# A two-layer streaming encoder on one core: x of the second layer brought into token form by VectorE block transposes and a copy through DRAM, where TensorE transposed it

## The chip, the cores and the metric

The kernel runs on one core of one Trainium2 chip. The core has engines that work side by side, each on its own list of instructions: TensorE (PE in the profile, with its weight loads as PEld), VectorE (DVE), ScalarE (ACT), GpSimd (POOL) and SyncE (SP), which here mostly issues DMA transfers. An engine runs its list in order, and an instruction that waits for another engine or a transfer holds up everything behind it on its own engine. The metric is the device time in microseconds (us) of one execution; lower is better. Where several times are given, the median counts.

## The reference, cut to what matters

The model has two layers on 272 tokens (16 learned ones and 256 of the input) of width 2048. Layer 0 mixes by gated linear attention and stick-breaking attention; layer 1, which the change touches, is a Mamba-2 block (SSD) with 8 groups of 8 heads of 64 channels. All is float32.

```python
proj = einsum('btd,de->bte', h, w_in)              # z, x, B, C and dt of layer 1
xbc = silu(causal_depthwise_conv(xbc, conv_w, conv_b))
dt = softplus(dt_raw + dt_bias)
xdt = x * dt[..., None]                            # per token and head
y = sum over s <= t of (C_t . B_s) * exp(a_cum_t - a_cum_s) * xdt_s   # computed by chunks there
y = rms_norm_groups((y + d_skip * x) * silu(z), norm_w)
out = einsum('bte,ed->btd', y, w_out)              # then residual and layer norm
```

The kernel computes the sum over s without chunks, as one causal matrix per head: M[s, t] = (C_t . B_s) exp(a_cum_t - a_cum_s) for s <= t, and y = xdt^T M. The contraction runs over tokens s, so TensorE wants xdt with tokens on the partitions.

## The kernel before, in words

**Weights and projections.** The weights come in 1 MB tiles `raw` (three buffers), each loaded by one SP transfer (L144) and split in two halves: ScalarE writes the high part `whi` (L159), VectorE, for some halves GpSimd, the low part `wlo` (L160); each has five buffers. A projection is a product of three fp32r matmuls per block (`three`, L178 to L180: high by high, high by low, low by high). A `unit` is 128 output channels of layer 1: 48 matmuls with 256 to 272 columns; the weights are the stationary side, so the result has channels on the partitions and tokens along the row. The output projection runs in units of 24 matmuls with 512 columns (L494 to L496).

**Order of layer 1.** For each group g the units are B, C, four of x and four of z; from group 2 on the four output units of group g-2 follow. Each unit's post-processing is pushed as a small generator task (`push`), and the tasks advance a step at a time between pieces of the projection (`tick`). Their `yield`s therefore decide how many steps later their instructions stand. A simulator of the framework then sets the order on every engine from the written program; all engines keep that order.

**x in a group.** `post_x` runs the convolution (ScalarE and three VectorE steps, L1046 and L1050) from PSUM into `xt` (channels by tokens, 4 blocks of 128 channels). After every second block, `x_path` runs silu (VectorE L1057, three ScalarE steps, VectorE L1061). After the second pair, 12 TensorE transposes follow: 8 of 128x128 (L1173) into two PSUM banks (`po`), and 4 of the last 16 tokens (L1177) into a third bank (`z`). VectorE then multiplies from PSUM by dt (held per token in `est`): four operations of 128x256 (L1186) into `xd`, and four of 16x128 (L1192) into `xd2`.

**The mix.** `mix_ssd` waits for all this and for M, and 32 matmuls (L1235) and 8 small ones (L1241) multiply `xd` by M into two `po` banks. `decay` forms M on VectorE and ScalarE from `ebc`, a copy of the group's cumulated decays on all partitions: 16 subtractions (L1105, L1106; called the M burst below), exponentials, and a product with C.B (L1133). `ebc` is a 1,664 KB transfer (L1072) into the one buffer of the tag `hacc`, so it is loaded once the M burst of the group before has ended. M(g+1)'s burst follows the mix of g.

Of the kernel before, what the change touches and what calls it, by code (L numbers as in the profile page):

```python
# [18 lines left out]
NFIRST = 6  # L19
T = NM + S  # L20
# [10 lines left out]
NG, HPG = 8, 8  # L31
# [51 lines left out]
def _wait(*tasks):  # L83
    for t in tasks:
        while not t.done:
            yield


class _Body:
# [904 lines left out]
    def dt_path(self, ps, scr):  # L994

        nc, lp = self.nc, self.lp
        act, vec = nc.scalar.activation, nc.vector
        H = 64
        while not self.normed:
            yield  # L1000
        m, e, s, s2, p = [scr[:H, i * T : (i + 1) * T] for i in range(5)]
        E = scr[:H, 5 * T : 5 * T + 432]
        bias = self.dta[:, 0:1]
        with self.tc.issue_after(self.last[0]):
            act(e, ps[:H, :T], AF.Abs, bias=bias)
        with self.tc.issue_after(self.last[1]):
            vec.tensor_scalar(m, ps[:H, :T], bias, 0.0, op0=ALU.add, op1=ALU.max)
        act(e, e, AF.Exp, scale=-1.0)

        vec.tensor_scalar(s2, e, 2.0, None, op0=ALU.add)  # L1010
        vec.reciprocal(s2, s2)
        vec.tensor_tensor(s, e, s2, op=ALU.mult)
        vec.tensor_tensor(s2, s, s, op=ALU.mult)
        yield
        vec.tensor_scalar(p, s2, 2.0 / 15, None, op0=ALU.mult)
        for c in (13, 11, 9, 7, 5, 3):
            vec.scalar_tensor_tensor(p, p, 2.0 / c, s2, op0=ALU.add, op1=ALU.mult)
        vec.scalar_tensor_tensor(p, p, 2.0, s, op0=ALU.add, op1=ALU.mult)
        vec.tensor_tensor(m, m, p, op=ALU.add)
        yield  # L1020
        na = lp.tile([H, 1], F32, tag="dt_na", name="dt_na")
        act(na, self.dta[:, 1:2], AF.Exp)
        vec.tensor_scalar(e, m, na, -1.0, op0=ALU.mult, op1=ALU.mult)
        vec.memset(s, 0.0)
        for o, t0 in ((0, 0), (272, 128), (416, 256)):
            vec.tensor_tensor_scan(E[:, o : o + T - t0], e[:, t0:T], s[:, t0:T], 0.0, op0=ALU.add, op1=ALU.add)
        self.edr = self.tc.dram_tile([H, 416], F32, name="edr")
        nc.sync.dma_start(self.edr, E[:, 16:432])
        yield
        self.est = lp.tile([P, 2, 2, H], F32, tag="est", name="est")  # L1030
        self.est2 = lp.tile([16, 2, H], F32, tag="est2", name="est2")
        yield from _wait(self.tasks["res"])
        pt = self.po()
        for n, a in enumerate((E[:, 0:128], E[:, 272:400], m[:, 0:128], m[:, 128:256])):
            nc.tensor.transpose(pt[:, n * H : (n + 1) * H], a, self.ident[:H, :H])
        for n, a in enumerate((E[:, 416:432], m[:, 256:272])):
            nc.tensor.transpose(pt[:16, 256 + n * H : 256 + (n + 1) * H], a, self.ident[:H, :H])
        vec.tensor_copy(self.est.rearrange("p a b h -> p (a b h)"), pt[:, :256])
        vec.tensor_copy(self.est2.rearrange("p a h -> p (a h)"), pt[:16, 256:384])
        yield  # L1040

    def conv(self, src, ct, v, t0=0, lo=0):
# [24 lines left out]
            self.load_decay(g)  # L1067

    def load_decay(self, g):
        eb = self.hp.tile([P, HPG, 416], F32, tag="hacc", name=self.nm("ebc"))  # L1070
        src = self.edr[g * HPG : (g + 1) * HPG, :].rearrange("h c -> (h c)").partition_broadcast(P)
        self.nc.sync.dma_start(eb.rearrange("p h c -> p (h c)"), src)  # L1072
        self.cur["ebc", g] = eb
# [5 lines left out]
    def decay1(self, g):  # L1079
        nc, lp = self.nc, self.lp  # L1080
        act, vec, mm = nc.scalar.activation, nc.vector, nc.tensor.matmul
# [20 lines left out]
        eb = self.cur["ebc", g]  # L1102
# [5 lines left out]
                act(M[:, h - 1 : h + 1, :], M[:, h - 1 : h + 1, :], AF.Exp)  # L1108
                yield
        mt = self.mt  # L1110
        e2 = self.est2[:, 0, g * HPG : (g + 1) * HPG].rearrange("p (h o) -> p h o", o=1).broadcast_to([16, HPG, 16])
        vec.tensor_tensor(mt, eb[:16, :, 400:416], e2, op=ALU.subtract)
        vec.tensor_scalar(mt, mt, 0.0, None, op0=ALU.min)
        act(mt, mt, AF.Exp)
# [5 lines left out]
        pin = self.tc.keep_in_program_order  # L1120
# [10 lines left out]
        for h in range(0, HPG, 2):  # L1131
            c = cb[:, 16:416].rearrange("p (o c) -> p o c", o=1).broadcast_to([P, 2, 400])
            vec.tensor_tensor(M[:, h : h + 2, :], M[:, h : h + 2, :], c, op=ALU.mult)  # L1133
            yield
        c = cb[:16, 0:16].rearrange("p (o c) -> p o c", o=1).broadcast_to([16, 2, 16])
# [16 lines left out]
    def x_path(self, g, j):  # L1152
        nc, vec = self.nc, self.nc.vector
        xt = self.cur["x", g]
        xd = self.cur["xd", g]
        self.silu1(xt[:, j : j + 2, :].rearrange("p a t -> p (a t)"), vec)
        yield
        yield
        yield
        if g == 0:  # L1160
            yield from _wait(self.tasks["dt"])
        if j == 0:
            return
        for _ in range(5):
            yield
        pin = self.tc.keep_in_program_order

        pts = [self.po(), self.po()]
        p2 = self.zbank()
        for pt, jj in zip(pts, (0, 2)):  # L1170
            for i in range(2):
                for t in range(2):
                    pin(nc.tensor.transpose(  # L1173
                        pt[:, t * 256 + i * P : t * 256 + (i + 1) * P], xt[:, jj + i, t * P : (t + 1) * P], self.ident
                    ))
        for i in range(4):
            pin(nc.tensor.transpose(p2[:16, i * P : (i + 1) * P], xt[:, i, 256:T], self.ident))  # L1177
        yield
        hv = lambda a: a.rearrange("p (h c) -> p h c", c=64)
        bd = lambda a: a.rearrange("p (h o) -> p h o", o=1)  # L1180
        for pt, jj in zip(pts, (0, 2)):
            h0 = g * HPG + 2 * jj
            c = slice(jj * P, jj * P + 256)
            for t in range(2):
                d = bd(self.est[:, 1, t, h0 : h0 + 4]).broadcast_to([P, 4, 64])
                vec.tensor_tensor(hv(xd[:, t, c]), hv(pt[:, t * 256 : (t + 1) * 256]), d, op=ALU.mult)  # L1186
            yield
        e2 = bd(self.est2[:, 1, g * HPG : (g + 1) * HPG])
        for j in range(2):
            for p in range(2):  # L1190
                h = 4 * p + 2 * j
                vec.tensor_tensor(  # L1192
                    self.xd2[32 * j : 32 * j + 16, 2 * p : 2 * p + 2, :], hv(p2[:16, :])[:, h : h + 2, :],
                    e2[:, h : h + 2, :].broadcast_to([16, 2, 64]), op=ALU.mult,
                )
        yield

    def post_z(self, ps, g, j):
# [260 lines left out]
```

## Time and profile before

| what | value |
|---|---|
| times of three runs | 1389.19, 1389.46, 1389.4 us; median 1389.4 us |
| the profiled execution | 1389.59 us; span 1387.7 us |
| granted TensorE clock | 1.0 throughout |
| PE busy | 1379.2 us, 99% of the span |
| PEld / DVE / ACT / POOL busy | 1328.3 (96%) / 1017.3 (73%) / 771.7 (56%) / 260.6 us (19%) |
| DMA | 249.83 MB, mean 180 GB/s; the SP queue's packets take 51.0% of 16 engines' span |
| layer 1 | from about 760 us to the end; its x paths run from 767 to 1316 us |

The span is the time between first and last instruction of the profiled execution; its own time is 1.9 us longer. Busy time counts from the start of an instruction to its end, and matmuls overlap, so that the distance between starts, not the duration of one, says what a matmul costs. In rows of groups, "xN" is the count, then busy us and mean ns of one, then the idle time of the engine just before the group's instructions. In rows of the timeline the first two columns are start and duration in us; "x4" joins neighbours; brackets hold the idle time before and what ended it.

### The profile page before, as it was taken

The numbers are of one execution on the slowest core, as the hardware profiler recorded it, in microseconds if no ns is written. First come the engines' busy times: TensorE is split into PE (matmuls) and PEld (weight loads), VectorE is DVE, ScalarE is ACT, GpSimd is POOL, SyncE is SP. The second block draws the span as 40 slices with busy tenths as digits, with TensorE's granted clock in tenths as the row PEclk, the third lists the DMA queues.
The fourth block names the chain that finished last, engine by engine and source line by source line (L and its number), as shares of the span: only waits on it lengthen the run. The fifth ranks groups of instructions, "written<-read, shape, count | busy, mean of one in ns | idle before, by whom it ended". The sixth has DMA issues, their size and how long they took to land.

```text
span 1387.7 us, 26097 instructions
## 1 busy us (share of the span) xinstructions
PE 1379.2 (99%) x10715; PEld 1328.3 (96%) x10715; DVE 1017.3 (73%) x1690; ACT 771.7 (56%) x1149; POOL 260.6 (19%) x253
## 2 busy tenths in 40 slices
PE   9999999999999999999999999999999999999998
PEld 8999999999999999999999999899898999989986
DVE  7857575574565565557899999787877778867687
ACT  6645454454345544556587677565565655656551
POOL 0000010100101000113500153331322323133221
PEclk9999999999999999999999999999999999999999
DMA  8544544445454445544354655465555556455561
GB/s 320 185 161 156 181 154 171 163 156 179 156 179 156 153 152 179 174 151 148 122 199 169 251 202 201 158 256 174 213 180 187 197 187 228 164 200 185 179 216 61
DMA packets 38007, 249.83 MB, mean 180 GB/s; under 512 B 4288, under 2 KB 6144, under 8 KB 9472
## 3 DMA queue, kind: packets, MB, share of 16 engines
q1 hardware_dynamic: 37168, 247.38, 51.0%
q8 instruction: 84, 1.38, 0.4%
q10 hardware_dynamic: 720, 0.79, 0.2%
q14 instruction: 35, 0.29, 0.1%
HBM read 245.94 MB, written 2.20 MB: 179 GB/s over the span
## 4 chain that ended last, share of the span: by engine, by line
PE 94%; DVE 3%; DMA 1%; ACT 1%; POOL 1%; issue 0%; SPq 0%; ACTq 0%; POOLq 0%; DVEq 0%
PE pj L179 25%; PE pj L178 25%; PE pj L180 25%; PE pj L494 4%; PE pj L496 4%; PE pj L495 4%; PE po L1235 1%; PE po L608 1%; DVE wlo L160 1%; PE po L1173 0%; DMA raw<-in_wts 0%; PE po L587 0%; PE z L1123 0%; POOL yu L1246 0%; DVE M L1105 0%
## 5 line engine op out<-in xcount | busy, mean ns | idle before, releaser
L178 PE MATMUL pj<-xhi,whi 128*128 128x272 f32 (+4 forms) x2560 | 732.1, 286 | 1.3 <-DVE fix L936 0.5
L179 PE MATMUL pj<-xlo,whi 128*128 128x272 f32 (+4 forms) x2560 | 730.8, 286 | 0.0
L180 PE MATMUL pj<-xhi,wlo 128*128 128x272 f32 (+4 forms) x2560 | 730.1, 286 | 0.0
L159 ACT ACTIVATE whi<-raw 128x1024 fp32r<-128x1024 f32 (+2 forms) x434 | 449.6, 1039 | 423.8 <-PE pj L179 350.7
L160 DVE TENSOR_TENSOR wlo<-raw,whi 128x1024 fp32r<-128x1024 f32 (+2 forms) x405 | 503.3, 1247 | 242.0 <-ACT whi L159 237.4
L178 PEld LDWEIGHTS pj<-xhi,whi 128*128 128x128 f32 x2560 | 482.1, 189 | 3.7 <-ACT whi L159 0.9
L179 PEld LDWEIGHTS pj<-xlo,whi 128*128 128x128 f32 x2560 | 482.1, 188 | 1.5 <-DVE wlo L160 0.4
L180 PEld LDWEIGHTS pj<-xhi,wlo 128*128 128x128 f32 x2560 | 481.9, 188 | 1.0 <-issue 0.8
L178 PE MATMUL pj<-mixh,whi 128*128 128x272 f32 x384 | 110.5, 289 | 0.0
L180 PE MATMUL pj<-mixh,wlo 128*128 128x272 f32 x384 | 110.5, 288 | 0.0
L179 PE MATMUL pj<-mixl,whi 128*128 128x272 f32 x384 | 110.4, 288 | 0.0
L160 POOL TENSOR_TENSOR wlo<-raw,whi 128x1024 fp32r<-128x1024 f32 x29 | 73.0, 2517 | 192.6 <-ACT whi L159 192.6
L494 PE MATMUL pj<-whi,yh 128*128 128x512 f32 (+1 forms) x240 | 93.3, 389 | 0.0
L495 PE MATMUL pj<-wlo,yh 128*128 128x512 f32 (+1 forms) x240 | 92.6, 386 | 0.0
L496 PE MATMUL pj<-whi,yl 128*128 128x512 f32 (+1 forms) x240 | 92.2, 386 | 0.0
L261 POOL TENSOR_TENSOR gr<-gr,gsc 128x1088 f32<-128x1088 f32 x6 | 15.4, 2568 | 308.2 <-ACT gsc L260 308.2
L179 PEld LDWEIGHTS pj<-mixl,whi 128*128 128x128 f32 x384 | 72.3, 188 | 0.2
L180 PEld LDWEIGHTS pj<-mixh,wlo 128*128 128x128 f32 x384 | 72.3, 188 | 0.1
L178 PEld LDWEIGHTS pj<-mixh,whi 128*128 128x128 f32 x384 | 72.2, 188 | 0.1
L503 DVE SCALAR_TENSOR_TENSOR acc<-pj,rr,acc 128x512 f32<-128x512 f32 (+1 forms) x65 | 46.5, 734 | 13.9 <-PE pj L496 13.9
L496 PEld LDWEIGHTS pj<-whi,yl 128*128 128x128 f32 x240 | 45.1, 188 | 9.1
L494 PEld LDWEIGHTS pj<-whi,yh 128*128 128x128 f32 x240 | 45.1, 188 | 9.0
(351 smaller groups left out, 1472.2 us busy)
## 6 DMA issues: line engine op xcount, KB each, us to landing
raw<-in_wts SPq DMA_DIRECT2D x212, 1024.0 KB, 4.8
ebc<-edr SPq DMA_DIRECT2D x8, 1664.0 KB, 6.7
raw<-in_wts SPq DMA_DIRECT2D x9, 256.0 KB, 6.4
hacc<-in_xT SPq DMA_DIRECT2D x7, 272.0 KB, 5.3
early<-in_wts SPq DMA_DIRECT2D x2, 512.0 KB, 6.5
lg<-in_lnr SPq DMA_DIRECT2D x1, 1024.0 KB, 4.7
lb<-in_lnr SPq DMA_DIRECT2D x1, 1024.0 KB, 5.3
out_h<-acc SPq DMA_DIRECT2D x2, 384.0 KB, 2.4
```

The source lines that it names most:

```text
L159: self.nc.scalar.activation(hi, src, AF.Copy)
L160: eng.tensor_tensor(lo, src, hi.bitcast(F32), op=ALU.subtract)
L178: mm(ps, whi, xhi, start=first, stop=False)
L179: mm(ps, whi, xlo, start=False, stop=False)
L180: mm(ps, wlo, xhi, start=False, stop=last)
L261: mul(c, c, e, op=ALU.mult)
L494: mm(ps, yh[:, kk, tt], hi[:, k, :], start=kk == 0, stop=False)
L495: mm(ps, yh[:, kk, tt], lo[:, k, :], start=False, stop=False)
L496: mm(ps, yl[:, kk, tt], hi[:, k, :], start=False, stop=kk == 3)
L503: self.nc.vector.scalar_tensor_tensor(a, ps, r[:, t : t + 1], a, op0=ALU.mult, op1=ALU.add)
L608: mm = lambda r, a, b, start=False, stop=False: self.nc.tensor.matmul(o[:, r], a, b, start=start, stop=stop, skip_group_check=True)
L1235: pin(mm(ov[p][i * 64 : (i + 1) * 64, jj, t0:S], xd[:, s, h * 64 : (h + 1) * 64], M[:, h, c0:c1], start=(s, jj) == (0, 0), stop=False, **gk,))
```

## The change

`x_path` no longer uses TensorE. After each pair's silu, VectorE transposes `xt` in blocks of 32x32, each within itself: one instruction for 256 tokens of two blocks (L1171, 128 partitions x 512 elements), and one for the columns of the last tokens (L1172, 128 x 64). A block's inside is then token by channel, but each block of 32 tokens still lies on the partitions of its channels. So SP writes the result to DRAM (L1179, 512 KB in rows of 4 KB; L1180, 64 KB) and reads it back with tokens on the partitions: four transfers of 128 KB in pieces of 512 bytes (L1183), two of 32 KB in pieces of 128 bytes straight into `xd2` (L1187). VectorE then multiplies by dt from SBUF: four operations of 128x4x64 (L1199), two of 16x256 in place on `xd2` (L1206).

The room for the blocks is the last 1,024 floats per partition of the buffer that holds `ebc`. So `x_path` waits until `ebc` of its group is allocated, and the load of `ebc` of the next group waits until L1199 has read the blocks back. The waits for dt and five `yield`s are gone. `est2` stands on two partition ranges. M, the mix and everything else is unchanged, though the lines are 1 to 11 numbers higher: L1061 is L1062, L1072 is L1075, L1105/L1106 are L1108/L1109, L1235/L1241 are L1246/L1252.

```diff
--- before.py
+++ after.py
@@ -1028,7 +1028,7 @@
         nc.sync.dma_start(self.edr, E[:, 16:432])
         yield
         self.est = lp.tile([P, 2, 2, H], F32, tag="est", name="est")
-        self.est2 = lp.tile([16, 2, H], F32, tag="est2", name="est2")
+        self.est2 = lp.tile([48, 2, H], F32, tag="est2", name="est2")
         yield from _wait(self.tasks["res"])
         pt = self.po()
         for n, a in enumerate((E[:, 0:128], E[:, 272:400], m[:, 0:128], m[:, 128:256])):
@@ -1036,7 +1036,8 @@
         for n, a in enumerate((E[:, 416:432], m[:, 256:272])):
             nc.tensor.transpose(pt[:16, 256 + n * H : 256 + (n + 1) * H], a, self.ident[:H, :H])
         vec.tensor_copy(self.est.rearrange("p a b h -> p (a b h)"), pt[:, :256])
-        vec.tensor_copy(self.est2.rearrange("p a h -> p (a h)"), pt[:16, 256:384])
+        for q in (0, 32):
+            vec.tensor_copy(self.est2[q : q + 16].rearrange("p a h -> p (a h)"), pt[:16, 256:384])
         yield
 
     def conv(self, src, ct, v, t0=0, lo=0):
@@ -1067,7 +1068,9 @@
             self.load_decay(g)
 
     def load_decay(self, g):
-        eb = self.hp.tile([P, HPG, 416], F32, tag="hacc", name=self.nm("ebc"))
+        eb = self.hp.tile([P, KT * T], F32, tag="hacc", name=self.nm("ebc"))
+        self.cur["xs", g] = eb[:, HPG * 416 :].rearrange("p (b c x) -> p b c x", c=4, x=32)
+        eb = eb[:, : HPG * 416].rearrange("p (h c) -> p h c", h=HPG)
         src = self.edr[g * HPG : (g + 1) * HPG, :].rearrange("h c -> (h c)").partition_broadcast(P)
         self.nc.sync.dma_start(eb.rearrange("p h c -> p (h c)"), src)
         self.cur["ebc", g] = eb
@@ -1108,7 +1111,7 @@
                 act(M[:, h - 1 : h + 1, :], M[:, h - 1 : h + 1, :], AF.Exp)
                 yield
         mt = self.mt
-        e2 = self.est2[:, 0, g * HPG : (g + 1) * HPG].rearrange("p (h o) -> p h o", o=1).broadcast_to([16, HPG, 16])
+        e2 = self.est2[:16, 0, g * HPG : (g + 1) * HPG].rearrange("p (h o) -> p h o", o=1).broadcast_to([16, HPG, 16])
         vec.tensor_tensor(mt, eb[:16, :, 400:416], e2, op=ALU.subtract)
         vec.tensor_scalar(mt, mt, 0.0, None, op0=ALU.min)
         act(mt, mt, AF.Exp)
@@ -1157,42 +1160,50 @@
         yield
         yield
         yield
-        if g == 0:
-            yield from _wait(self.tasks["dt"])
+        while ("ebc", g) not in self.cur:
+            yield
+
+        xs = self.cur["xs", g]
+        lp = self.lp
+        if j == 0:
+            self.cur["x9", g] = lp.tile([P, 4, 32], F32, tag="x9", name=self.nm("x9"))
+        x9 = self.cur["x9", g]
+        vec.transpose(xs[:, :, j : j + 2, :].rearrange("p b c x -> p c b x"), xt[:, j : j + 2, :S].rearrange("p c (b x) -> p c b x", x=32))
+        vec.transpose(x9[:, j : j + 2, :], xt[:, j : j + 2, 240:T])
+        yield
         if j == 0:
             return
-        for _ in range(5):
-            yield
-        pin = self.tc.keep_in_program_order
-
-        pts = [self.po(), self.po()]
-        p2 = self.zbank()
-        for pt, jj in zip(pts, (0, 2)):
+
+        d = self.tc.dram_tile([4, 32, 8, P], F32, name=self.nm("xdr"))
+        d9 = self.tc.dram_tile([4, 32, 4, 32], F32, name=self.nm("xdr9"))
+        nc.sync.dma_start(d.rearrange("p t b x -> (p t) (b x)"), xs.rearrange("q b c x -> q (b c x)"))
+        nc.sync.dma_start(d9.rearrange("p t c x -> (p t) (c x)"), x9.rearrange("q c x -> q (c x)"))
+        xb = xs.rearrange("q b c x -> q (b c x)").rearrange("q (s p x) -> q s p x", s=2, p=4)
+        for b in range(4):
+            nc.sync.dma_start(
+                xb[32 * b : 32 * b + 32], d[:, :, b::4].rearrange("p t s x -> t s p x")
+            )
+        for i in range(2):
+            nc.sync.dma_start(
+                self.xd2[32 * i : 32 * i + 16].rearrange("t (n a) (b x) -> t n (a b) x", n=2, b=2),
+                d9[:, 16:, i::2].rearrange("p t n x -> t n p x"),
+            )
+        yield
+        yield
+
+        for t in range(2):
             for i in range(2):
-                for t in range(2):
-                    pin(nc.tensor.transpose(
-                        pt[:, t * 256 + i * P : t * 256 + (i + 1) * P], xt[:, jj + i, t * P : (t + 1) * P], self.ident
-                    ))
-        for i in range(4):
-            pin(nc.tensor.transpose(p2[:16, i * P : (i + 1) * P], xt[:, i, 256:T], self.ident))
-        yield
-        hv = lambda a: a.rearrange("p (h c) -> p h c", c=64)
-        bd = lambda a: a.rearrange("p (h o) -> p h o", o=1)
-        for pt, jj in zip(pts, (0, 2)):
-            h0 = g * HPG + 2 * jj
-            c = slice(jj * P, jj * P + 256)
-            for t in range(2):
-                d = bd(self.est[:, 1, t, h0 : h0 + 4]).broadcast_to([P, 4, 64])
-                vec.tensor_tensor(hv(xd[:, t, c]), hv(pt[:, t * 256 : (t + 1) * 256]), d, op=ALU.mult)
-            yield
-        e2 = bd(self.est2[:, 1, g * HPG : (g + 1) * HPG])
-        for j in range(2):
-            for p in range(2):
-                h = 4 * p + 2 * j
-                vec.tensor_tensor(
-                    self.xd2[32 * j : 32 * j + 16, 2 * p : 2 * p + 2, :], hv(p2[:16, :])[:, h : h + 2, :],
-                    e2[:, h : h + 2, :].broadcast_to([16, 2, 64]), op=ALU.mult,
-                )
+                o = xd[:, t, :].rearrange("q (c i a x) -> q c i a x", c=4, i=2, a=2)[:, :, i]
+                x = xb[:, t, 2 * i : 2 * i + 2].rearrange("q a (c x) -> q c a x", c=4)
+                e = self.est[:, 1, t, g * HPG + i : (g + 1) * HPG : 2].rearrange("q (c o u) -> q c o u", o=1, u=1)
+                vec.tensor_tensor(o, x, e.broadcast_to([P, 4, 2, 32]), op=ALU.mult)
+            yield
+        for i in range(2):
+            q = slice(32 * i, 32 * i + 16)
+            x = self.xd2[q].rearrange("t (n h) c -> t n h c", n=2)
+            e = self.est2[q, 1, g * HPG : (g + 1) * HPG].rearrange("t (n j h) -> t j n h", n=2, j=2)[:, i]
+            e = e.rearrange("t n (h u) -> t n h u", u=1)
+            vec.tensor_tensor(x, x, e.broadcast_to([16, 2, 2, 64]), op=ALU.mult)
         yield
 
     def post_z(self, ps, g, j):
```

What this moves is shown at three places. First TensorE in group 3, within the unit of the block `pj`, before:

```order
L180 MATMUL pj_11389<-xhi,wlo_11331 128x256
L1173 MATMUL po_11406<-ident,xt_11029 128x128 x4
L1173 MATMUL po_11407<-ident,xt_11029 128x128 x4
L1177 MATMUL z_64<-ident,xt_11029 16x128 x4
L178 MATMUL pj_11389<-xhi,whi_11330 128x256
```

and with the change at the same place of that unit:

```order
L180 MATMUL pj_11406<-xhi,wlo_11334 128x256
L178 MATMUL pj_11406<-xhi,whi_11333 128x256
L179 MATMUL pj_11406<-xlo,whi_11333 128x256
L180 MATMUL pj_11406<-xhi,wlo_11334 128x256
L178 MATMUL pj_11406<-xhi,whi_11333 128x256
```

The 12 transposes are gone from the middle of the unit, and nothing stands in their place.

Second, VectorE in group 3 from the second silu on (L1061 before, L1062 now; L160 are weight splits, L1057/L1058 begin the silu of z). Before:

```order
L1061 TENSOR_TENSOR xt_11029<-xt_11029,xcl_11279 128x544
L160 TENSOR_TENSOR wlo_11441<-raw_11327,whi_11440 128x1024
L160 TENSOR_TENSOR wlo_11479<-raw_11387,whi_11478 128x1024
L1057 TENSOR_SCALAR xcl_11420<-gz_11325 128x512
L1186 TENSOR_TENSOR xd_11030<-po_11406,est 128x256 x2
L1186 TENSOR_TENSOR xd_11030<-po_11407,est 128x256 x2
L1192 TENSOR_TENSOR xd_8126<-z_64,est_8718 16x128 x4
L160 TENSOR_TENSOR wlo_11507<-raw_11387,whi_11506 128x1024
L160 TENSOR_TENSOR wlo_11540<-raw_11475,whi_11539 128x1024
L160 TENSOR_TENSOR wlo_11587<-raw_11535,whi_11586 128x1024
```

With the change:

```order
L1062 TENSOR_TENSOR xt_11027<-xt_11027,xcl_11280 128x544
L1171 STREAM_TRANSPOSE ebc_10878<-xt_11027 128x2x8x32
L1172 STREAM_TRANSPOSE x_1359_11185<-xt_11027 128x64
L160 TENSOR_TENSOR wlo_11476<-raw_11404,whi_11475 128x1024
L1058 TENSOR_SCALAR xcl_11425<-gz_11328 128x512
L160 TENSOR_TENSOR wlo_11504<-raw_11404,whi_11503 128x1024
L160 TENSOR_TENSOR wlo_11537<-raw_11472,whi_11536 128x1024
L1199 TENSOR_TENSOR xd_11028<-ebc_10878,est 128x4x64 x4
L1206 TENSOR_TENSOR xd_8126<-xd_8126,est_8718 16x256 x2
L160 TENSOR_TENSOR wlo_11584<-raw_11532,whi_11583 128x1024
L1058 TENSOR_SCALAR xcl_11546<-gz_11328 128x512
```

The two transposes stand right behind the silu, and three weight splits later the multiplies; the split behind them is queued after whatever they wait for.

On SP the same stretch now reads (`raw` are weight tiles, `xdr` the copies in DRAM, and L1187's target is `xd2`); before there were only weight tiles in it:

```order
L144 DMA raw_11532<-in_wts 128x2048
L1179 DMA xdr_11349<-ebc_10878 128x1024
L1180 DMA xdr_1379_11350<-x_1359_11185 128x128
L144 DMA raw_11579<-in_wts 128x2048
L1183 DMA ebc_10878<-xdr_11349 32x8x128 x4
L1187 DMA xd_8126<-xdr_1379_11350 16x8x32 x2
L144 DMA raw_11661<-in_wts 128x2048
L1075 DMA ebc_11821<-edr 128x3328
L144 DMA raw_11707<-in_wts 128x2048
```

A weight tile stands between the write and the reads, another behind the reads, and then comes the decay copy of group 4, which stood far ahead of these rows before.

Third, VectorE in group 1, with the change, behind the second transposes and up to the multiplies (L1051 are steps of a convolution, L266 to L268 a row statistic):

```order
L160 TENSOR_TENSOR wlo_10026<-raw_9873,whi_10025 128x1024
L266 TENSOR_TENSOR rt_9435<-rr_9436 128x2
L1051 SCALAR_TENSOR_TENSOR bc_9866<-pj_9800,cpk,bc_9866 128x270
L267 SCALAR_TENSOR_TENSOR rt_9435<-rt_9435,rm_9434 128x2
L1051 SCALAR_TENSOR_TENSOR bc_9866<-pj_9800,cpk,bc_9866 128x269
L268 SCALAR_TENSOR_TENSOR rr_9436<-rt_9435,rr_9436 128x2
L160 TENSOR_TENSOR wlo_10063<-raw_9980,whi_10062 128x1024
L1051 SCALAR_TENSOR_TENSOR bc_9866<-pj_9875,cpk,bc_9866 128x256 x3
L1058 TENSOR_SCALAR xcl_10007<-bc_9866 128x528
L1199 TENSOR_TENSOR xd_9242<-ebc_9081,est 128x4x64 x4
L1206 TENSOR_TENSOR xd_8126<-xd_8126,est_8718 16x256 x2
```

The multiplies stood in front of the splits of `raw_9873` and the steps of this convolution before; now they are behind both, and the mix of group 1 stands about two and a half units later on TensorE than before.

More of the change, by code (lines that the diff above doesn't have):

```diff
@@ L1162, in x_path @@
+        yield
         if j == 0:
             return
-        for _ in range(5):
-            yield
-        pin = self.tc.keep_in_program_order
-        pts = [self.po(), self.po()]
-        p2 = self.zbank()
-        for pt, jj in zip(pts, (0, 2)):
-            for i in range(2):
-                for t in range(2):
-                    pin(nc.tensor.transpose(
-                        pt[:, t * 256 + i * P : t * 256 + (i + 1) * P], xt[:, jj + i, t * P : (t + 1) * P], self.ident
-                    ))
@@ new lines, in x_path @@
+        yield
[6 more added lines that the diff above has]
+                vec.tensor_tensor(o, x, e.broadcast_to([P, 4, 2, 32]), op=ALU.mult)
+            yield
+        for i in range(2):
+            q = slice(32 * i, 32 * i + 16)
[3 more added lines that the diff above has]
+            vec.tensor_tensor(x, x, e.broadcast_to([16, 2, 2, 64]), op=ALU.mult)
```

## The prediction

> **What bounds the kernel now.** I read the page first: the busy times and the chain of waits.
>
> ```profile
> PE 1379.2 (99%) x10715; PEld 1328.3 (96%) x10715; DVE 1017.3 (73%) x1690; ACT 771.7 (56%) x1149; POOL 260.6 (19%) x253
> PE 94%; DVE 3%; DMA 1%; ACT 1%; POOL 1%; issue 0%; SPq 0%; ACTq 0%; POOLq 0%; DVEq 0%
> ```
>
> TensorE is busy for 99% of the span and is 94% of the chain that ends last, so what leaves TensorE's list should leave the time, as long as nothing else takes its place. Since shares are averages, the second view is the table of busy time by window (columns: length, then PE, PEld, DVE, ACT, POOL, granted clock, DMA share, GB/s). Groups 0 to 2 form their x in the first of these windows, groups 3 to 7 in the second.
>
> ```profile
> 760.00:900.00 140.00, 139.79 (x1139) 131.90 (x1139) 127.80 (x244) 93.52 (x143) 47.91 (x35) 1.00 0.57 202
> 900.00:1340.00 440.00, 440.00 (x3269) 412.73 (x3268) 336.97 (x518) 258.11 (x360) 123.75 (x93) 1.00 0.56 195
> ```
>
> TensorE has no gap in either, at full clock. VectorE has 12.2 us free of 140 in the first and 103 of 440 in the second. The early stretch is therefore where VectorE could become the bound, and it gets work from this change.
>
> **What leaves TensorE.** The timeline of PE around group 3's transposes (start, duration, then the line):
>
> ```profile
> 956.38 1.04 PE L1173 MATMUL po<-ident,xt 128*128 128x128 f32 x8
> 957.25 0.60 PE L1177 MATMUL z<-ident,xt 128*16 128x128 f32 x4
> 957.61 0.37 PE L178 MATMUL pj<-xhi,whi 128*128 128x256 f32 x1
> 957.81 0.28 PE L179 MATMUL pj<-xlo,whi 128*128 128x256 f32 x1
> 957.93 0.28 PE L180 MATMUL pj<-xhi,wlo 128*128 128x256 f32 x1
> ```
>
> Matmuls overlap, so I count from start to start. From 956.38 to 957.81 there are 12 transposes and one L178; a matmul of this unit is worth 957.93 - 957.81 = 0.12 us. The transposes cost 1.43 - 0.12 = 1.31 us, and eight groups 10.5 us. Bounds: the pitch alone, (957.25 - 956.38) / 8 = 0.109 us, times 96 is 10.4 us; where a group's transposes stand in two places, the slow step behind them (957.81 - 957.61 - 0.12 = 0.08 us) comes twice, 11.1 us in all. I take 10.5 us.
>
> **What VectorE loses and gets.** Its timeline in group 3, from the second silu to the M burst, brackets being idle time:
>
> ```profile
> 954.05 0.73 DVE L1061 TENSOR_TENSOR xt<-xt,xcl 128x544 f32<-128x544 f32 x1 [0.37 <-ACT xcl L1060]
> 957.67 1.41 DVE L1186 TENSOR_TENSOR xd<-po,est 128x256 f32<-128x256 f32 x4
> 959.00 0.96 DVE L1192 TENSOR_TENSOR xd<-z,est 16x128 f32<-16x128 f32 x4
> 960.25 1.23 DVE L160 TENSOR_TENSOR wlo<-raw,whi 128x1024 fp32r<-128x1024 f32 x1 [0.29 <-ACT whi L159]
> 963.01 1.23 DVE L160 TENSOR_TENSOR wlo<-raw,whi 128x1024 fp32r<-128x1024 f32 x1 [1.54 <-ACT whi L159]
> 968.40 1.23 DVE L160 TENSOR_TENSOR wlo<-raw,whi 128x1024 fp32r<-128x1024 f32 x1 [4.16 <-ACT whi L159]
> 971.25 1.23 DVE L160 TENSOR_TENSOR wlo<-raw,whi 128x1024 fp32r<-128x1024 f32 x1 [1.29 <-ACT whi L159]
> 977.11 0.35 DVE L1105 TENSOR_SCALAR M<-ebc,est 128x256 f32<-128x256 f32 x1 [1.49 <-PE po L1235]
> 983.08 1.21 DVE L160 TENSOR_TENSOR wlo<-raw,whi 128x1024 fp32r<-128x1024 f32 x1
> ```
>
> L1186 and L1192 leave: 1.41 + 0.96 = 2.4 us. For what comes, the nearest rows are groups by shape (count, busy us, mean ns):
>
> ```profile
> L1057 DVE TENSOR_SCALAR xcl<-gz 128x512 f32<-128x512 f32 x16 | 6.7, 419 | 0.0
> L1061 DVE TENSOR_TENSOR xt<-xt,xcl 128x544 f32<-128x544 f32 x15 | 12.3, 820 | 11.9 <-ACT xcl L1060 11.7
> L1105 DVE TENSOR_SCALAR M<-ebc,est 128x256 f32<-128x256 f32 x64 | 30.0, 469 | 7.0 <-PE po L1235 7.0
> ```
>
> No block transpose is in the trace. One of 128x512 should lie between 0.42 us (L1057, as many elements) and 0.82 us (L1061); I take 0.5, two are 1.0 us. The two of 64 columns I take at 0.2 each, below the 0.24 us of one L1192 (0.96 / 4). The four L1199 have 256 elements like L1186, 0.35 to 0.47 us each; at 0.4, 1.6 us. Two L1206 at 0.35, 0.7 us. Together 3.7 us, bounds 3.0 and 4.9. VectorE gets 1.3 us more per group (0.6 to 2.5). In groups 3 to 7 that costs nothing: the idle times in brackets above are 9.1 us in this one group. Without that cover it would be 1.3 us of time per group.
>
> [...]
>
> **The way through DRAM, on the clock of group 3.** The durations come from the DMA issues (KB each, median us from issue to landing), the deadlines from PE and SP rows:
>
> ```profile
> raw<-in_wts SPq DMA_DIRECT2D x212, 1024.0 KB, 4.8
> ebc<-edr SPq DMA_DIRECT2D x8, 1664.0 KB, 6.7
> raw<-in_wts SPq DMA_DIRECT2D x9, 256.0 KB, 6.4
> out_h<-acc SPq DMA_DIRECT2D x2, 384.0 KB, 2.4
> edr<-dt_scr SPq DMA_DIRECT2D x1, 104.0 KB, 2.1
> ```
>
> ```profile
> 974.13 2.93 PE L1235 MATMUL po<-M,xd 128*64 128x256 f32 x32
> 983.18 0.33 SPq L1072 DMA_DIRECT2D ebc<-edr  x1
> 988.59 0.39 PE L495 MATMUL pj<-wlo,yh 128*128 128x512 f32 x1
> ```
>
> - The silu ends at 954.05 + 0.73 = 954.8; the second transposes (0.5 + 0.2) at 955.5.
> - The write of 512 KB takes between 2.4 us (`out_h`, 384 KB) and 6.4 us (256 KB behind others). I take 4.0, nearer to half a weight tile: 959.5, at the latest 961.9.
> - The reads stand behind a weight tile on SP. Its buffer is freed by the split at 960.25, so it leaves at 961.5, and the reads right behind it.
> - Six reads bring 576 KB. Alone, 2.1 us (`edr`). In turn, each with its own 2.1 us behind a tile of 4.8 us, 17.4 us. I take them as bytes in the stream of the tile: (1024 + 576) / 1024 x 4.8 = 7.5 us, because weight tiles of 1 MB land in 4.8 us though the DMA engines are busy 0.56 of that window. They land at 969.0 (963.6 to 979.3).
> - L1199 and L1206 take 2.3 us: xd is ready at 971.3. The mix starts at 974.1: 2.8 us to spare; at the upper end 7.5 us late.
>
> Queued behind L1199 on VectorE is a weight split. It would have started at 968.40 and now starts at 971.3, 2.9 us late. The tightest split I quote, that at 983.08, ends at 984.3 and is first used by TensorE at 988.59, 4.3 us later. So the wait is covered, by 1.4 us; once the cover is gone each us is one on TensorE. On SP, behind the reads, wait weight tiles and then the decay copy of group 4, which now also waits for L1199 (end 970.6): it lands at 970.6 + 6.7 = 977.3, and the M burst that needs it began at 977.11. Before, a copy left at 983.18, at the end of one burst, for a burst a whole group later. The burst, and the split at 983.08 behind it, come 0.2 us late, up to 2 us if the copy shares with a tile; both within the 4.3 us. I cost groups 3 to 7 at nothing, and I see that two covers are thin.
>
> **Groups 0 to 2.** Here VectorE has 12.2 / 3 = 4.1 us free per group, and it must take 1.3 us of work and the same sort of wait at L1199, up to the 2.9 us of group 3: 4.2 us. That just does not fit. The mixes of groups 0 and 1 stand later on TensorE, which takes the pressure off xd but not off the splits. Bounds: no loss, and three waits of 2.9 us uncovered, 8.7 us. I take 1.5 us, since before these waits there are more splits in VectorE's order than in group 3, and a later wait is a shorter one.
>
> **Sum.** The profiled execution took 1389.59 us, span 1387.7 us and 1.9 us around it, 0.2 us over the median of 1389.4. 1389.59 - 10.5 + 1.5 = 1380.6; against the median, 1380.4 us.
>
> **Rivals.**
>
> *VectorE keeps half of the early stretch.* For it: 91% busy there. Against it: the wait falls behind more work. Half of 8.7 us: 1389.4 - 10.5 + 4.35 = 1383.3 us.
>
> *The gain is eaten.* All three early waits are uncovered (8.7 us) and the thin covers of groups 3 to 7 give a little: 1389.4 - 10.5 + 8.7 = 1387.6 us and up to 1392, no difference that counts.
>
> *The round trip is late at every mix: slower.* The place is L1199, behind the reads on SP. TensorE's list reaches the mix, xd is not there, and the eight mixes each wait. It decides from 10.5 / 8 = 1.3 us late per group, that is, when the reads land 4.1 us later than I take them. Half way between my value (2.8 us early) and the upper end (7.5 us late) is 2.4 us late: 1389.4 - 10.5 + 8 x 2.4 = 1398.1 us; by the upper end, 1439. For it: the reads are in pieces of 512 and 128 bytes where weight tiles come in rows of 8 KB, and 256 KB of weights took 6.4 us while 1 MB took 4.8, so bytes are not what always decides. Against it: six transfers that are issued at once need not run in turn.
>
> [...]
>
> *The change doesn't do what it says.* The orders of PE exclude it: the transposes are gone and nothing is added.
>
> **Chances and range.** A difference under 0.2% (2.8 us) can't be told from none. My forecast (1378 to 1382.5) 0.47, the half loss 0.17, the gain eaten 0.09, slower 0.24. Below 1378, with the 11.1 us bound and nothing lost early, 0.03. So faster 0.03 + 0.47 + 0.17 = 0.67, within 0.2% 0.09, slower 0.24. Up to 1395 the slower case is half included, so the range 1378 to 1395 leaves out 0.12 above and 0.03 below. The likeliest's own range is 1378 to 1382.5.
>
> **What would show it.** PE rows without L1173 and L1177, and no gap ahead of L1246 in any group: then the sum holds. In the waits, PE L1246 waiting for L1199 or L1206 by over 1 us shows the slower rival. The split behind L1199 and the idle time that VectorE spends before L1199 show the size of the wait; I expect about 3 us in groups 3 to 7. M bursts that begin later than the mix's end with a DMA of `ebc` as their releaser show the second thin cover. PE idle before L180 (released by `wlo`) between 760 and 900 shows the early loss. My number is wrong if the reads take over 11 us, or if VectorE's transposes take over 1.5 us each.

## The result

The changed kernel takes 1396.1 us (median; 1392.1 to 1400.8), the kernel before 1389.24 us (1388.6 to 1390.1) in runs beside it. The ratio is 1.0054, interval 1.0038 to 1.0070: slower by 6.9 us, where 9 us less were forecast. Besides, the time now varies by nearly 9 us from run to run; before it varied by 1.5 us.

The profiled execution is the fastest of the changed kernel's, 1392.13 us (span 1390.2 us), 2.5 us over the one of before. Its page, busy times and chain:

```profile
PE 1371.7 (99%) x10619; PEld 1321.0 (95%) x10619; DVE 1029.6 (74%) x1707; ACT 771.7 (56%) x1149; POOL 254.8 (18%) x253
PE 87%; DVE 6%; DMA 4%; issue 1%; ACT 1%; POOL 0%; SPq 0%; ACTq 0%; DVEq 0%; POOLq 0%
```

The transposes did leave: TensorE has 96 instructions fewer and is busy for 7.5 us less. But it is 87% of the chain where it was 94%; VectorE has grown from 3% to 6% of it and DMA from 1% to 4%. By window, as in the prediction:

```profile
760.00:900.00 140.00, 134.53 (x1082) 127.53 (x1082) 126.13 (x232) 89.81 (x137) 36.89 (x32) 0.99 0.65 219
900.00:1340.00 440.00, 434.80 (x3217) 407.14 (x3216) 347.38 (x542) 259.29 (x361) 126.97 (x95) 1.00 0.61 210
```

TensorE, with a gap of 0.2 us in all before, now stands still for 5.5 us in the first window and 5.2 us in the second. The timeline of PE holds it in five waits (the bracket is the wait and what ended it):

```profile
816.91 0.40 PE L178 MATMUL pj<-xhi,whi 128*128 128x272 f32 x1 [1.76 <-ACT gz L1213]
841.75 0.62 PE L1246 MATMUL po<-M,xd 128*64 128x256 f32 x2 [2.30 <-DVE xd L1199]
893.80 3.17 PE L1246 MATMUL po<-M,xd 128*64 128x256 f32 x32 [1.41 <-DVE xd L1199]
908.65 0.47 PE L494 MATMUL pj<-whi,yh 128*128 128x512 f32 x1 [2.27 <-DVE acc L503]
1079.32 0.47 PE L494 MATMUL pj<-whi,yh 128*128 128x512 f32 x1 [2.93 <-DVE acc L503]
```

They sum to 10.7 us. Two of the five are waits for x at a mix, as the prediction's slower rival has them. The first is for ScalarE, which has to empty a PSUM bank of z; the last two are for VectorE, which has to empty a bank of the output projection.

There is a further loss that the waits don't show. Windows around 842 us:

```profile
838.00:842.00 4.00, 1.70 (x14) 1.42 (x12) 0.82 (x3) 2.41 (x4) 1.30 (x1) 1.00 0.88 282
842.00:846.00 4.00, 4.00 (x21) 2.31 (x20) 3.94 (x7) 0.00 (x0) 0.00 (x0) 0.57 0.63 216
846.00:850.00 4.00, 4.00 (x44) 3.74 (x40) 2.57 (x7) 1.16 (x3) 1.43 (x2) 1.00 0.97 403
```

Right after the wait of 2.30 us TensorE's granted clock is 0.57 for 4 us, by which I estimate another 4 x 0.43 = 1.7 us: the last 30 matmuls of this mix take 4.46 us, all 32 of group 2's 3.17. So 1389.59 - 10.5 + 10.7 + 1.7 = 1391.5 us, near the 1392.13 us of this execution. It is the only one with a trace, so the 4.0 us from it to the median are not accounted for; the mean clock does not order the times, since three executions at 0.999 took 1394.1 to 1395.0 us, five at 0.995 or 0.996 took 1396.1 to 1400.8, and this one had 0.998.

**Where each wait comes from.** First the one at 816.91, followed back over VectorE, GpSimd and ScalarE:

```profile
808.96 0.46 DVE L1256 SCALAR_TENSOR_TENSOR yu<-xt,cpk,po 128x256 f32<-128x256 f32 x1
809.57 3.53 POOL L1257 TENSOR_TENSOR yu<-yu,gz 128x256 f32<-128x256 f32 x1 [6.45 <-DVE yu L1256]
813.14 0.51 ACT L1259 ACTIVATE yh<-yu,cpk 128x256 fp32r<-128x256 f32 x1 [3.16 <-POOL yu L1257]
816.50 0.88 ACT L1213 ACTIVATE gz<-pj 128x256 f32<-128x256 f32 x3
```

After group 0's mix VectorE computes yu, late, since its list is full (from 795 to 820 us it has no idle time); GpSimd and then ScalarE wait for it in their lists; the emptying of z's banks stands behind that on ScalarE; TensorE has no free bank. No transfer is in this chain. But L1257 on GpSimd also takes 3.53 us where 0.74 is its median: the 2.8 us more are longer than the wait at the end of the chain, and why it took so long was not tested. Next the mix of group 1, on SP and VectorE:

```profile
825.63 0.33 SPq L1179 DMA_DIRECT2D xdr<-ebc  x1
832.36 3.34 SPq L1183 DMA_DIRECT2D ebc<-xdr  x4
841.17 1.43 DVE L1199 TENSOR_TENSOR xd<-ebc,est 128x256 f32<-128x256 f32 x4 [5.11 <-DMA ebc<-xdr]
```

The write leaves at 825.63, the reads at 832.36, the multiplies start at 841.17: 15.5 us. VectorE waits 5.1 us for them, with its list full behind. Last the wait at 908.65, by way of the decay copy:

```profile
894.69 0.33 SPq L1075 DMA_DIRECT2D ebc<-edr  x1
901.25 2.36 DVE L1108 TENSOR_SCALAR M<-ebc,est 128x256 f32<-128x256 f32 x1 [1.33 <-DMA ebc<-edr]
907.77 1.39 DVE L503 SCALAR_TENSOR_TENSOR acc<-pj,rr,acc 128x512 f32<-128x512 f32 x2
```

The copy for group 3 leaves when L1199 of group 2 has ended (894.69), the M burst waits for it until 901.25, and the evictions L503 stand behind the burst. TensorE needs their bank. This wait is thus made by the change in group 2; only the one at 1079.32 is made by a later group.

### The profile page after: what moved, and what is told of

Its sections match the earlier page's. It is cut to its first block, busy times and chain, and to the rows that moved or that the text cites. A ratio compares the mean times of both kernels' runs of the same rounds, so it can differ in the third digit from the quotient of the medians.

```text
span 1390.2 us, 25999 instructions
## 1 busy us (share of the span) xinstructions
PE 1371.7 (99%) x10619; PEld 1321.0 (95%) x10619; DVE 1029.6 (74%) x1707; ACT 771.7 (56%) x1149; POOL 254.8 (18%) x253
## 4 chain that ended last, share of the span: by engine, by line
PE 87%; DVE 6%; DMA 4%; issue 1%; ACT 1%; POOL 0%; SPq 0%; ACTq 0%; DVEq 0%; POOLq 0%
PE pj L179 24%; PE pj L178 24%; PE pj L180 24%; PE pj L494 3%; PE pj L496 3%; PE pj L495 3%; PE po L608 1%; DMA ebc<-xdr 1%; PE po L1246 1%; DMA ebc<-edr 1%; DMA xdr<-ebc 1%; DVE wlo L160 1%; DVE M L1108 1%; DVE M L1109 0%; POOL yu L1257 0%
## 5 line engine op out<-in xcount | busy, mean ns | idle before, releaser
L180 PE MATMUL pj<-xhi,wlo 128*128 128x272 f32 (+4 forms) x2560 | 729.6, 285 | 0.0
L160 DVE TENSOR_TENSOR wlo<-raw,whi 128x1024 fp32r<-128x1024 f32 (+2 forms) x405 | 504.8, 1250 | 226.4 <-ACT whi L159 225.3
L180 PEld LDWEIGHTS pj<-xhi,wlo 128*128 128x128 f32 x2560 | 482.0, 188 | 0.3
L180 PE MATMUL pj<-mixh,wlo 128*128 128x272 f32 x384 | 110.5, 288 | 0.0
L160 POOL TENSOR_TENSOR wlo<-raw,whi 128x1024 fp32r<-128x1024 f32 x29 | 74.5, 2569 | 168.2 <-ACT whi L159 168.2
L180 PEld LDWEIGHTS pj<-mixh,wlo 128*128 128x128 f32 x384 | 72.3, 188 | 0.1
L495 PEld LDWEIGHTS pj<-wlo,yh 128*128 128x128 f32 x240 | 45.1, 188 | 8.6
```

The source lines that it names most:

```text
L160: eng.tensor_tensor(lo, src, hi.bitcast(F32), op=ALU.subtract)
L180: mm(ps, wlo, xhi, start=False, stop=last)
L495: mm(ps, yh[:, kk, tt], lo[:, k, :], start=False, stop=False)
```

## The experiments

All times are medians; ratios are to the kernel before, run beside. In every run the simulator sets the order of all engines anew, so an edit can also move instructions that it does not touch.

**1. The transposes alone.** The kernel before without them; VectorE multiplies x as it lies:

```diff
-        pts = [self.po(), self.po()]
-        p2 = self.zbank()
...
-        vec.tensor_tensor(hv(xd[:, t, c]), hv(pt[:, t * 256 : (t + 1) * 256]), d, op=ALU.mult)
+        vec.tensor_tensor(f(hv(xd[:, t, c])), x, f(d), op=ALU.mult)   # x is a part of xt
```

> The kernel before, with the 12 transposes of every group left out and nothing put in their place: VectorE multiplies x as it lies (channels on the partitions), so x reaches the mix untransposed. It measures the first term of the prediction alone. By the prediction's rows the transposes cost 10.5 us (bounds 10.4 to 11.1), so 1389.2 - 10.5 = 1378.7 us (1378 to 1379.5). If the PE time that leaves is taken up again by another engine (VectorE in the early groups, weights), it comes out above 1382 us, and the loss in the changed kernel would not be the transfers' alone.

1382.9 us (1380.2 to 1384.2; ratio 0.9953, 0.9938 to 0.9967). The gain is 6.3 us, not 10.5, though no work was added to any engine. Its waits of PE:

```profile
PE po L1250 <- POOL ysq L1244: 1.8, 1, 1.8
PE pj L178 <- ACT gz L1191: 0.7, 1, 0.7
```

Both lie between 815 and 830 us, where TensorE stands still for 2.56 us and the granted clock is 0.77 on the mean:

```profile
815.00:830.00 15.00, 12.44 (x74) 11.82 (x74) 13.47 (x21) 11.69 (x23) 4.39 (x4) 0.77 0.61 210
```

By that I estimate at most 15 x 0.23 = 3.45 us more. TensorE is faster by itself in the early groups and runs into the engines that follow it. The gain went with the mean clock: of the four executions the shortest, at 1.0, gained 9.0 us, the longest, at 0.998, 5.0 us.

**2. No way through DRAM.** The changed kernel without write, read back and the last tokens:

```diff
-        nc.sync.dma_start(d.rearrange(...), xs.rearrange(...))
-        nc.sync.dma_start(d9.rearrange(...), x9.rearrange(...))
...
-        for b in range(4):
-            nc.sync.dma_start(xb[32 * b : 32 * b + 32], d[:, :, b::4].rearrange("p t s x -> t s p x"))
```

> The changed kernel with the way through DRAM left out: no write, no read back; VectorE transposes the blocks and multiplies them where they lie, so x reaches the mix with its blocks unmoved and the last tokens are left out. Theory: the changed kernel loses its gain to waits for the way through DRAM (TensorE at the mixes of groups 1 and 2, and the decay copy that waits for the multiplies, so the M burst and then the evictions of the output units come late). Without the transfers 1378 to 1382 us. Rival: VectorE's own new work (transposes of 0.70 us where 0.5 was expected) makes it the bound in the early groups: then 1386 us or more, with TensorE waiting for VectorE between 800 and 910 us.

1389.7 us (ratio 1.0004, 0.9994 to 1.0013): nothing is gained, so my theory of the transfers fell. The rival held in its time, but TensorE waits for ScalarE and not for VectorE itself. The one large wait of PE, and what stands behind it on GpSimd and ScalarE:

```profile
PE pj L178 <- ACT gz L1200: 9.2, 1, 9.2
```

```profile
819.39 1.57 POOL L1244 TENSOR_TENSOR yu<-yu,gz 128x256 f32<-128x256 f32 x1 [10.85 <-DVE yu L1243]
825.35 1.21 ACT L1200 ACTIVATE gz<-pj 128x256 f32<-128x256 f32 x4 [3.54 <-POOL yu L1244]
```

It is the wait of 816.91 again, now 9.2 us long, with VectorE's yu at its root. Without a single transfer the early groups eat the whole gain of eight groups.

**3. The decay copy parted from the blocks.** One lasting buffer, of which `ebc` and the blocks are two parts, so that the copy no longer waits for L1199:

```diff
-        eb = self.hp.tile([P, KT * T], F32, tag="hacc", name=self.nm("ebc"))
+        if g == 0:
+            self.eball = self.hp.tile([P, KT * T], F32, tag="hacc", name="ebc")
+        eb = self.eball
```

> The changed kernel with ebc and the blocks as two parts of one lasting buffer, so that the decay copy of group g+1 waits only for the M burst of group g, as in the kernel before, and no longer for L1199; all else as changed. Theory: the two waits of TensorE for evictions (L494 for L503, 2.3 and 2.9 us in the profile) go, the two at the mixes of groups 1 and 2 (2.3 and 1.4 us) stay: 5.2 us less than the changed kernel's 1396.1, so about 1391 us (1388 to 1393). Rival, that these waits come from VectorE's load or from DMA traffic in general: no change, 1395 to 1397 us.

1394.4 us (1392.4 to 1397.6; ratio 1.0037, 1.0026 to 1.0049). That is 1.7 us less than the changed kernel, but the intervals overlap, and it lies above the expected range. The wait for evictions falls from 5.2 to 1.4 us, while the wait behind ScalarE is 6.1 us here; alone the run doesn't settle the price of the copy.

**4. The change in groups 3 to 7 alone.**

```diff
-            self.tasks["x", g, j] = self.push(self.x_path(g, j - 1))
+            self.tasks["x", g, j] = self.push((self.x_path_old if g < 3 else self.x_path)(g, j - 1))
```

> The change in groups 3 to 7 alone; groups 0 to 2 use TensorE as before. Theory: five eighths of the 10.5 us leave (6.6 us), the waits at 817, 842, 894 and 909 us in the profile go, that at 1079 us (2.9 us) stays: 1389.2 - 6.6 + 2.9 = 1385.5 us (1383 to 1389). Rival, that the loss is spread over all eight groups: five eighths of the whole loss of 6.9 us, 1393.5 us.

1386.5 us (1383.0 to 1390.8; ratio 0.9982, 0.9971 to 0.9992): faster than before by 2.6 us, as expected. The profiled execution, at 1390.8 us the longest of the ten, waits twice for evictions:

```profile
PE pj L494 <- DVE acc L503: 5.0, 2, 2.5
```

**5. The same with the decay copy parted** (the edits of 3 and 4 together).

> The change in groups 3 to 7 alone, and the decay copy parted from the blocks, so that it waits for the M burst of the group before alone. Theory: what the change in groups 3 to 7 alone still loses (1386.5 us against 1389.2 - 6.6 = 1382.6) is the late decay copy: two waits of TensorE of 2.5 us for evictions behind the M burst, and the lowered clock behind each. Parted, 1382.5 to 1384 us. Rival, that the loss is in DMA traffic or in the wait at L1199: it stays at 1386 us or more.

1383.9 us (1382.7 to 1384.8; ratio 0.9961, 0.9946 to 0.9976). This beats both kernels: 5.5 us under the one before. Its wait for evictions, and the early window:

```profile
PE pj L494 <- DVE acc L503: 2.7, 2, 1.6
```

```profile
760.00:900.00 140.00, 140.00 (x1138) 132.08 (x1137) 127.78 (x246) 94.27 (x145) 45.68 (x35) 1.00 0.56 201
```

TensorE is full again in the early window. The copy's late start costs about 2.7 us in groups 3 to 7 (1386.5 - 1383.9; the intervals of the two overlap a little). Not all waits for evictions go with it: 2.7 of 5.0 us stay in these two executions.

**6. Groups 3 to 7 alone, without the way through DRAM** (2 and 4 together).

> The change in groups 3 to 7 alone, and there without the way through DRAM (x reaches the mix with its blocks unmoved, the last tokens are left out). Theory: outside the early groups VectorE's extra work is hidden and the whole PE time leaves: 1382 to 1383.5 us. The difference to the change in groups 3 to 7 alone (1386.5 us) is then the price of the transfers. Rival, that VectorE's work costs time here too: over 1385 us.

1381.9 us (1381.3 to 1382.0; ratio 0.9946, 0.9931 to 0.9961). The gain is 7.4 us where five eighths of 10.5 us are 6.6: all of it, with VectorE's transposes and multiplies in place, and a little more than expected (the interval, 5.4 to 9.6 us, holds both). So in these groups VectorE's work is hidden, and the transfers cost 1386.5 - 1381.9 = 4.6 us, of which the copy is 2.7.

**7. The change in groups 0 to 2 alone** (the condition of 4 turned round).

> The change in groups 0 to 2 alone. Theory: here lies the loss, since VectorE is full: 3.9 us of PE time leave, but the waits between 815 and 910 us and the clock behind them come, 8 to 12 us: 1393 to 1398 us. Rival, that the loss is spread evenly over the groups: 1389.2 + 3/8 x 6.9 = 1391.8 us or less.

1397.8 us (1395.5 to 1398.6; ratio 1.0059, 1.0044 to 1.0074), 8.5 us slower than before and as slow as the full change. The waits at 817, 841, 893 and 908 us are all there, and none behind them.

**8. VectorE's transposes added to the kernel before, in groups 0 to 2.** TensorE's transposes stay; nobody reads the new result; no transfer:

```diff
+        if g < 3:
+            while ("ebc", g) not in self.cur:
+                yield
+            vec.transpose(self.xs[:, :, j : j + 2, :].rearrange("p b c x -> p c b x"), xt[:, j : j + 2, :S].rearrange("p c (b x) -> p c b x", x=32))
...
+            vec.transpose(self.x9[:, j : j + 2, :], xt[:, j : j + 2, 240:T])
```

> The kernel before, with TensorE's transposes kept, and in groups 0 to 2 VectorE's block transposes added beside them with nobody reading the result: 3 x 1.8 = 5.4 us of VectorE time, no transfer. Theory: in the early groups VectorE is so full that this alone makes TensorE wait and lowers its clock: 1392 to 1398 us. Rival, that only the transfers and the moved mixes cost time: within 1.5 us of 1389.2 us.

1395.95 us (1395.4 to 1396.6; ratio 1.0047, 1.0030 to 1.0064). 5.4 us of VectorE time, with the orders that the simulator made of it, cost 6.6 us. The wait of PE is the known one:

```profile
PE pj L178 <- ACT gz L1212: 4.8, 1, 4.8
```

**9. The same in groups 3 to 7** (`g >= 3`).

> The kernel before, with TensorE's transposes kept, and in groups 3 to 7 VectorE's block transposes added beside them with nobody reading the result: 5 x 1.8 = 9.0 us of VectorE time, where 5.4 us in groups 0 to 2 cost 6.6 us. Theory: here VectorE waits for weights anyway, so it costs nothing: 1388.8 to 1390 us. Rival, that VectorE's work costs time anywhere: 1395 us or more.

1389.6 us (1389.2 to 1389.9; ratio 1.0004, 0.9994 to 1.0013). 9.0 us of VectorE time cost nothing, by the same edit. Place, not amount, decides.

**10 and 11. VectorE relieved in groups 0 to 2.** Three VectorE steps of x's convolution are left out there, once in the kernel of 3, once in the kernel before:

```diff
-        self.conv(ps, 4 * g + j, xt[:, j, :])
+        self.conv(ps, 4 * g + j, xt[:, j, :], taps=() if g < 3 else (1, 2, 3))
```

> The change with the decay copy parted from the blocks (1394.4 us), and VectorE relieved in groups 0 to 2: the three VectorE steps of x's convolution are left out there (12 x 3 steps of 0.49 us, 17.6 us), so x is computed from one tap in these groups. Theory: the loss of the early groups is VectorE's queue, so it goes: 1389.3 - 10.5, plus about 2 us for the transfers of groups 3 to 7 and up to 2 for those of groups 0 to 2: 1381 to 1384 us. Rival, that the transfers or the moved mixes make the early loss: 1391 us or more.

> The kernel before with the same relief of VectorE in groups 0 to 2 (three steps of x's convolution left out there). Theory: TensorE has no gap before, so nothing is gained: 1388.5 to 1389.5 us. If it falls by more than 1 us, the relief itself is worth time, and the run beside it must be read against it.

With the change 1380.4 us (1379.8 to 1381.5; ratio 0.9939, 0.9924 to 0.9953); before 1388.7 us (ratio 0.9995, 0.9986 to 1.0004). The relief is worth nothing to the kernel before, and 14 us to the changed one with the copy parted (1394.4 to 1380.4). With it the change gains 8.3 us, transfers and all, a little more than the expected range allowed. The early window of the changed one:

```profile
760.00:900.00 140.00, 139.35 (x1118) 131.19 (x1116) 121.34 (x220) 91.90 (x138) 38.25 (x33) 1.00 0.64 225
```

**12. The change from group 2 on, copy parted.**

> The change in groups 2 to 7, decay copy parted. Theory: group 2 is at the end of the full stretch; if VectorE's work fits there, its 1.3 us of PE time come on top of 1383.9 us: 1382.6 us (1381.5 to 1384). If the early stretch reaches to group 2, TensorE waits at its mix as in the changed kernel (1.4 us at 894, then 2.3 us at 909): 1385 to 1388 us.

1384.9 us (1383.4 to 1386.7; ratio 0.9971, 0.9961 to 0.9982), no better than from group 3 on, and not told apart from it by the intervals. The 1.3 us that leave TensorE in group 2 do not show.

## Why the prediction was wrong

**What failed: groups 0 to 2.** The step reads that VectorE "has 12.2 / 3 = 4.1 us free per group" there, and takes a loss of 1.5 us, at most 8.7. The 12.2 us were an average over 140 us. Shorter windows of the kernel before show where they lie:

```profile
780.00:800.00 20.00, 20.00 (x169) 17.72 (x168) 19.95 (x48) 11.87 (x17) 2.73 (x1) 1.00 0.70 253
800.00:815.00 15.00, 14.79 (x128) 14.36 (x127) 14.83 (x23) 12.34 (x23) 9.77 (x10) 1.00 0.65 243
815.00:830.00 15.00, 15.00 (x139) 13.96 (x139) 14.88 (x27) 8.93 (x15) 6.03 (x2) 1.00 0.51 162
830.00:850.00 20.00, 20.00 (x166) 20.00 (x165) 19.89 (x38) 15.53 (x26) 11.14 (x9) 1.00 0.65 234
```

From 780 to 850 us VectorE is busy for 69.55 of 70 us. It is as full as TensorE; both set the pace. Time that leaves TensorE there was worth nothing at the median (experiment 1: 6.3 us gained in eight groups, and five of them alone are worth 6.6), and time that VectorE gets is paid in full (8). The rows were there to be read; I read the mean.

The size, from the runs: without transfers, the change in all groups takes 1389.7 us, in groups 3 to 7 alone 1381.9. Groups 0 to 2 thus cost 7.8 us where they should have gained 3.9: 11.8 us without a single transfer. The transfers cost 6.4 us in all (1396.1 - 1389.7), 4.6 of it in groups 3 to 7, so 1.8 early, if the parts add up. The sum, put right: 1389.3 - 10.5 + 11.8 + 1.8 + 4.6 = 1397 us, measured 1396.1. Its last three terms are taken from these runs and from 1396.1 itself, so it is bookkeeping and no test. Experiment 7, which is not in it, has the early groups lose 8.5 + 3.9 = 12.4 us. My 1.5 us should have been 12 to 14 (13.6 by the sum), and the bound was of the wrong kind: I priced waits of VectorE at L1199, while the loss is mostly that its list became longer, and that ScalarE and GpSimd wait for it in order. The experiments do not part the longer list from the orders that the simulator made of it: in experiment 8 TensorE's transposes of group 1 start at 828.82 us, before at 811.39.

**Also too low: groups 3 to 7 "at nothing".** The copy was foreseen 0.2 to 2 us late, with 4.3 us of cover behind the M burst, read from a weight split. But the evictions L503 also stand behind the burst, and their cover is thinner. In groups 3 to 7 TensorE waited there once in the changed kernel (2.93 us) and twice in experiment 4 (2.5 us each), and in layer 1 never for a weight split. Group 2 shows the same step: the copy left at 894.69 and the burst could only begin at 901.25. In these terms groups 3 to 7 lost 4.6 us (experiments 4 and 6), where I had none; 2.7 of them go when the copy is parted, and the other 1.9 are the rest of the way through DRAM, whose waits were not followed further.

**What held.** The transposes' term: experiment 6 gives 7.4 us for five groups where rows said 6.6, and with VectorE relieved the change gains 8.3 us, with about 2 lost to transfers in groups 3 to 7 (1383.9 - 1381.9, experiments 5 and 6). VectorE's extra work was just in bounds; groups by shape after the change:

```profile
L1199 DVE TENSOR_TENSOR xd<-ebc,est 128x256 f32<-128x256 f32 x32 | 15.9, 556 | 29.4 <-DMA ebc<-xdr 29.4
L1171 DVE STREAM_TRANSPOSE ebc<-xt 128x512 f32<-128x512 f32 x16 | 11.3, 705 | 0.1
L1206 DVE TENSOR_TENSOR xd<-xd,est 16x256 f32<-16x256 f32 x16 | 6.6, 410 | 0.2
L1172 DVE STREAM_TRANSPOSE x<-xt 128x64 f32<-128x64 f32 x16 | 3.2, 200 | 0.0
```

Per group that is 2 x 0.705 + 2 x 0.200 + 4 x 0.556 + 2 x 0.410 = 4.9 us, at the upper bound of 4.9, where 3.7 was taken; less the 2.4 us that leave, 2.5 instead of 1.3. A large transpose took 0.705 us where I took 0.5.

The transfers, us from issue to landing:

```profile
xdr<-ebc SPq DMA_DIRECT2D x8, 512.0 KB, 5.5
ebc<-xdr SPq DMA_DIRECT2D x32, 128.0 KB, 4.7
```

The write took 5.5 us where I took 4.0. The reads run together and not in turn, as my sum had it: they leave SP some 0.6 us apart, and each takes 4.7. The shortest took 2.6 us; six reads in turn at 2.1 us each, the upper end on which the slower rival rests, do not show.

**The signs it named.** PE idle before L180, for a low half of the weights, was to show the early loss; there is no such wait. The idle time of VectorE before L1199 was expected at about 3 us in groups 3 to 7 and was 2.80 to 5.31 us. The number was to be wrong if the reads took over 11 us or a transpose over 1.5 us. Where VectorE waited for the reads they took at most 8.9 us from the first issue, and a transpose took 0.71 us; the number was wrong all the same. These signs watch the new instructions, and the loss was in the lists that they joined.

**The rivals.** The slower one, the way through DRAM late at all eight mixes, gave the right sign for the wrong reason: TensorE waited for x at two mixes only, both early. That its 1398.1 us lies 2 us from the measured time is luck. The one that named the mechanism, VectorE in the early stretch, was given 0.17 and a price of 4.35 us, a third of what it cost.

## What to carry to other kernels

Before work is moved to an engine, its busy share belongs in windows of 10 to 20 us at the very place where the work arrives; 91% over 140 us hid 70 us at 99%. Where two engines were both full here, taking time from one gave nothing at the median (6.3 us in eight groups, 6.6 foreseen for five of them alone), and giving time to the other cost all of it (6.6 us for 5.4). The same change is worth 2.6 us when it is kept to the groups in which VectorE has room, and 5.5 us when the decay copy is parted from the blocks as well. The buffer that is shared here to save space also shared its waits, at about 2.7 us in groups 3 to 7, and the cover behind the delayed M burst was that of the evictions queued behind it (TensorE waited 2.27 and 2.93 us for them), not that of the weight split from which I read 4.3 us.

## What the runs showed of the hardware

TensorE's granted clock was lower behind some waits of little more than 2 us: a mean of 0.57 over 4 us after 2.30 us (842 us), and 0.63 after 2.50 us in the change of groups 3 to 7 alone:

```profile
1072.00:1076.00 4.00, 4.00 (x12) 3.15 (x13) 4.00 (x6) 1.51 (x2) 0.00 (x0) 0.63 0.72 262
```

After waits of 2.27 and 2.93 us in the changed kernel it stayed at 1.00, so length alone did not decide; what did was not shown. Where the clock fell, a wait cost more than its length, by my estimates from clock and time: 1.7 us more at 842 us, at most 3.45 us in experiment 1 (a mean of 0.77 from 815 to 830 us, with waits of 0.7 and 1.8 us), and about 2.03 x 0.50 + 4 x 0.25 = 2.0 us in experiment 8, with its wait of 4.8 us:

```profile
820.00:824.00 4.00, 2.03 (x9) 2.03 (x10) 3.07 (x8) 2.46 (x7) 1.92 (x2) 0.50 0.88 307
824.00:828.00 4.00, 4.00 (x27) 4.00 (x27) 2.00 (x2) 2.14 (x5) 0.59 (x1) 0.75 0.15 61
```

In experiment 4 the three executions with a mean clock of 1.0 took 1383.0 to 1384.6 us, the seven with 0.997 or 0.998 took 1386.1 to 1390.8; so a large part of what the late copy costs there may be the clock. This was not tried by itself.

SP spent 3.34 us on issuing the four reads at 832.36 (a median of 0.61 us for one of the 32), while a weight tile or the write takes 0.33 us. Some VectorE and GpSimd instructions took far longer than usual while the other engine was at work: the split L160 on VectorE at 825.95 took 2.32 us where 1.23 is the median, L1257 on GpSimd at 809.57 took 3.53 us where 0.74 is. I did not test the cause.
